# Another order of a unit's seven products in the last projection and in the unit in front of it, and the first block's sample matmuls in groups of four

## The chip, the cores and the metric

The kernel runs on one core of a Trainium2 chip. The metric is the device time of one execution in microseconds (us). One core has five engines that run side by side, each with its own queue of instructions: TensorE (PE, matrix products), VectorE (DVE), ScalarE (ACT), GpSimd (POOL) and SyncE (SP, which here issues most transfers). They wait for one another through semaphores. Matrix products are accumulated in banks of PSUM; everything else lies in SBUF, which has 128 partitions.

## The reference: what is computed

One inference step of one decoder layer, in fp32, for a prompt of 2048 tokens and, with the same weights, for 32 sample tokens (8 sequences of 4). The model width is 1024, the hidden width of the feed-forward part 2816.

```python
def decoder_layer(x, s_gla, s_ssm, conv_buf, mk, mv, lw):
    m, s_gla, s_ssm, conv_buf = mixer(rmsnorm(x, lw['ln_mix_pre']), s_gla, s_ssm, conv_buf, lw)
    h = x + rmsnorm(m, lw['ln_mix_post'])
    a = cross_attend(rmsnorm(h, lw['ln_xa_pre']), mk, mv, lw['w_xq'], lw['w_xo'])
    h = h + rmsnorm(a, lw['ln_xa_post'])
    hf = rmsnorm(h, lw['ln_ffn_pre'])
    f = (jax.nn.silu(hf @ lw['w_gate']) * (hf @ lw['w_up'])) @ lw['w_down']
    h = h + rmsnorm(f, lw['ln_ffn_post'])
    return h, s_gla, s_ssm, conv_buf
```

`mixer` is one large projection (`hn @ w_in`), gated linear attention on one half of the channels, a state-space scan (SSD, with a decay per head and chunk) on the other, and an output projection. `cross_attend` attends over 256 memory tokens. The outputs are both groups of tokens and the new states.

## The kernel before

**Products.** Every fp32 product is made of three matmuls on halves: each operand is split into a high part (a rounded copy, made by ScalarE) and a low part (the rest, a subtraction on VectorE), and `three` (lines 133 to 136) adds high x high (line 134), high x low (135) and low x high (136) into one PSUM bank.

**First half (0 to 857 us).** Four blocks of 512 tokens go through the input projection, the attention heads and the scan. `wload` (line 120) loads a raw piece of weights of 128 x 1024 on SP's queue into one of two `wraw` buffers and splits it into `whi` and `wlo`. `tm(n)` is one of three projections with tokens in the rows: four weight pieces (`u`), each with 24 matmuls of 512 columns. In the first block (`has_s`) the 32 sample tokens ride along: behind each piece come two sample matmuls, which take the raw, unsplit weights, and which lie in different column groups of TensorE (`tile_position=(0, g0)`):

```python
                if has_s:
                    for kk in range(2):
                        kt = 2 * u + kk
                        g0 = (kt % 4) * 32
                        nc.tensor.matmul(psv[g0:g0 + 32], lhsT=sx[:, kt], rhs=wr[:, kk * 512:(kk + 1) * 512],
                                         start=kt < 4, stop=kt >= 4, tile_position=(0, g0))
```

The scan's running decays are transposed into a tile of 16 rows (`lcT`) and spread by a mask (`bmask`) into rows 0 to 15 of an operand `R`, by GpSimd. `junk` is a scratch tile that takes squares whose sums alone are wanted.

**Second half (857 to 2833 us).** Here stand the other projections as passes over units: o, s and v (attention, 8 units each), three passes g (gate and up projection, 22 units each; the third with two row tiles and the samples, 272 columns), and three passes d (the last projection, 8 units each: parts of 3, 4 and 4 pairs of row tiles of the hidden width, so 384, 512 and 512 columns wide). GD is the first d pass, XG the first g pass.

A unit is a 2 x 2 block product by seven products instead of eight (Strassen and Winograd's form). Product 0 is p0, 1 is C11, 2 is p2, 3 is p3, 4 is C22, 5 is C12, 6 is C21; p0, p2, C22 and C21 go to the two buffers of bank `accA`, C11 to `accB`, p3 and C12 to `accC`. Their order is TURN = [0, 1, 3, 2, 5, 4, 6], and a list `order`, written out once, holds all products of all units. The last product of a unit stands behind the first of the next one, but ahead of it where XG or GD begins:

```python
    for n, (k, _, _) in enumerate(work):
        first = [(n, 0)]
        if n:
            first.insert(0 if begins[n] and k in (XG, GD) else 1, (n - 1, 6))
        order += first + [(n, i) for i in TURN[1:6]]
```

- *The moving side of a unit.* Its raw tile is loaded two units ahead (`load_unit`). Four products ahead of a product its operand is prepared: `Unit.hi` makes the sums S1, S2, S4 and S3 on VectorE (line 1644) where a product needs one (S1 with product 1, though product 3 reads it), the high part on ScalarE (line 1662); the low part (VectorE, line 1664) follows one product later.
- *The weights of a pass.* `Pieces` brings them in pieces of one or two per product, in the order of `flat`, which follows TURN. A piece is loaded into a staging buffer `st` (three of them), split on ScalarE (line 1731) and VectorE (line 1735), and lies in one of seven rooms of a ring, one room per product, taken in turn. A room is taken again only once the product of the pass before that lies in it is through in that pass's last unit (`inside`, `spent`; `larger` returns without work otherwise). One piece is made per product beside the last unit of the pass before, and then beside the first unit of the new one; a product whose weights are not there makes them first (`while i not in held[n].full: held[n].step()`).
- *Evictions.* What a product leaves in PSUM is copied or added into rows in SBUF: g passes at line 1991 (with ScalarE at line 1984 for the sigmoid part), d passes in `evac_d` (VectorE, line 2038, or a copy on ScalarE). In a d pass a row tile's store, or in the last part its final norm, is issued when the later one of its halves is there: for the first half of the rows (m = 0) at C12, for the second at C21.
- In the first unit of GD, eight sample matmuls at a time stand between two products (line 2082).

Of the kernel before, what the change touches and what calls it, by code (L numbers as in the profile page):

```python
# [12 lines left out]
F32 = mybir.dt.float32  # L13
F32R = mybir.dt.float32r
I32 = mybir.dt.int32
AF = mybir.ActivationFunctionType
# [26 lines left out]
def hymba_kernel(ctx: ExitStack, tc: tile.TileContext, a: dict, o: dict, dbg: dict | None = None):  # L43
# [17 lines left out]
    def mxt():  # L61
        return mx.tile([P, 512], F32, name="mx")
# [55 lines left out]
    last = [None]  # L118

    def wload(src, pieces=1, pool=None, raws=None):  # L120
        raw = (raws or wp).tile([P, 1024], F32, name="wraw", bufs=2)
        nc.sync.dma_start(out=raw, in_=src)
        hi, lo = ((pool or wp).tile([P, 1024], F32R, name=n, bufs=1 if pool else 3) for n in ("whi", "wlo"))
        w = 1024 // pieces
        with tc.high_priority(offset=AHEAD):
            for c in range(pieces):
                cs = slice(c * w, (c + 1) * w)
                last[0] = nc.scalar.activation(hi[:, cs], raw[:, cs], AF.Copy)  # L128
                nc.vector.tensor_tensor(lo[:, cs], raw[:, cs], f(hi)[:, cs], op=ALU.subtract)  # L129
        return raw, hi, lo  # L130
# [200 lines left out]
    nc.vector.memset(Sg, 0.0)  # L331
    Ss = pstate.tile([P, 512], F32, name="Ss")
    nc.vector.memset(Ss, 0.0)
    bmask = pstate.tile([16, 8], F32, name="bmask")
    nc.vector.tensor_tensor(bmask, ident[:16, 0:8], ident[:16, 8:16], op=ALU.add)
    sps = pstate.tile([96, BT], F32R, name="sps")
    nc.gpsimd.memset(f(sps), 0.0)
    rmask = pstate.tile([P, BT], F32, name="rmask")
# [183 lines left out]
    def block(b):  # L522
# [31 lines left out]

        def fm_narrow(u):

            raw = wp.tile([P, 1024], F32, name="wraw", bufs=2)
            nc.sync.dma_start(out=raw, in_=a["w_in_fm"][u])
            both = wp.tile([P, 1024], F32R, name="whi", bufs=3)
            nc.scalar.activation(both, raw, AF.Copy)  # L560
            k_c = lambda t: t.rearrange("p (k c) -> p k c", c=P)
            nc.vector.tensor_tensor(k_c(both)[:, :, 64:104], k_c(raw)[:, :, 0:40], k_c(f(both))[:, :, 0:40], op=ALU.subtract)
            pss = [acct() for _ in segs]
            for kt in range(KT):
                for si, (n0, n1) in enumerate(segs):
                    for part, x in enumerate((xh, xl)):
                        nc.tensor.matmul(pss[si][:, :n1 - n0], lhsT=both[:, kt * P:(kt + 1) * P], rhs=x[kt][:, n0:n1],
                                         start=kt == 0 and part == 0, stop=kt == KT - 1 and part == 1)
            return pieces(pss)
# [24 lines left out]
                beside()  # L594


        sp = pa.tile([40, BT], F32, name="sp")
        for pp, lo, hi, of_s in fm_narrow(12):
            dst = s_sp if of_s else sp[:, lo:hi]
            nc.scalar.copy(dst, pp[0:40])  # L600
            nc.vector.tensor_tensor(dst, pp[64:104], dst, op=ALU.add)
            if has_s:
                nc.vector.tensor_tensor(dst, dst, rb[:40, BT:T] if of_s else rb[:40, lo:hi], op=ALU.mult)
# [8 lines left out]
        lc, ll = lcl[:, 0:32], lcl[:, 32:64]  # L612
        wl_ = pa.tile([P, 96], F32, name="wl_")
        wdec, ell, elc = (wl_[:, 32 * i:32 * i + 32] for i in range(3))
        lcT = pa.tile([16, BT], F32, name="lcT")

        def decays():
            ps = mxt()
# [64 lines left out]
        def tm(n):  # L683

            ps = [acct() for i in range(4)]
            psv = mxt() if has_s else None
            for u in range(4):
                wr, wh, wl = wload(a["w_in_tm"][n, u])
                for i in range(4):
                    for kk in range(2):  # L690
                        kt = 2 * u + kk
                        three(ps[i], xh[kt][:, i * P:(i + 1) * P], xl[kt][:, i * P:(i + 1) * P],
                              wh[:, kk * 512:(kk + 1) * 512], wl[:, kk * 512:(kk + 1) * 512], kt == 0, kt == KT - 1)
                    if i % 2 == 0 and "pa2" not in late:
                        step(back)
                if has_s:
                    for kk in range(2):
                        kt = 2 * u + kk
                        g0 = (kt % 4) * 32
                        nc.tensor.matmul(psv[g0:g0 + 32], lhsT=sx[:, kt], rhs=wr[:, kk * 512:(kk + 1) * 512], start=kt < 4, stop=kt >= 4,  # L700
                                         tile_position=(0, g0))
                if u < 3:
                    beside(False)
            return ps, psv
# [59 lines left out]
        def ssd_first(c):  # L764
            cs = slice(c * CH, (c + 1) * CH)

            R = Rs[0]
            nc.gpsimd.tensor_tensor(out=R[0:16], in0=lcT[:, cs].unsqueeze(1).broadcast_to([16, 8, CH]),
                                    in1=bmask.unsqueeze(2).broadcast_to([16, 8, CH]), op=ALU.mult)
            M = pa.tile([P, 8, CH], F32, name="M")  # L770

            px = mxt()
# [32 lines left out]
        def ssd_second(c, M, xdt, xw, xD, Bt):  # L805
            cs = slice(c * CH, (c + 1) * CH)
            pi = mxt()
            for g in range(2):
                nc.tensor.matmul(pi[:, g * 256:(g + 1) * 256], lhsT=xc[6 + g][:, cs], rhs=Ss[:, g * 256:(g + 1) * 256], start=True, stop=True)
            py = mxt()  # L810
            for h in range(8):
                nc.tensor.matmul(py[:, h * 64:(h + 1) * 64], lhsT=M[:, h], rhs=xdt[:, h * 64:(h + 1) * 64], start=True, stop=True)
            y = pa.tile([P, 512], F32, name="y")
            nc.vector.tensor_tensor(v3(y), v3(pi), elc[:, c * 8:(c + 1) * 8].unsqueeze(2).broadcast_to([P, 8, 64]), op=ALU.mult)
            nc.gpsimd.tensor_tensor(out=xD, in0=xD, in1=y, op=ALU.add)
            nc.vector.tensor_tensor(xD, py, xD, op=ALU.add)
            y = z_[:, c]
            nc.gpsimd.tensor_tensor(out=y, in0=xD, in1=y, op=ALU.mult)

            pS = mxt()  # L820
            for g in range(2):
                nc.tensor.matmul(pS[:, g * 256:(g + 1) * 256], lhsT=Bt[:, g * P:(g + 1) * P], rhs=xw[:, g * 256:(g + 1) * 256], start=True, stop=True)
            nc.vector.tensor_tensor(v3(Ss), v3(Ss), ell[:, c * 8:(c + 1) * 8].unsqueeze(2).broadcast_to([P, 8, 64]), op=ALU.mult)
            nc.vector.tensor_tensor(Ss, Ss, pS, op=ALU.add)

            ss = small.tile([P, 8], F32, name="ss")
            for g in range(2):
                junk = pa.tile([P, 256], F32, name="junk")
                nc.scalar.activation(junk, y[:, g * 256:(g + 1) * 256], AF.Square, accum_out=ss[:, g:g + 1])
            rs = rstd_of(ss[:, 0:2], "rs", 256, cols=2)  # L830
            for g in range(2):
                nc.vector.tensor_scalar(y[:, g * 256:(g + 1) * 256], y[:, g * 256:(g + 1) * 256], rs[:, g:g + 1], None, op0=ALU.mult)
            return y
# [794 lines left out]

    TURN = [0, 1, 3, 2, 5, 4, 6]

    class Unit:

        def __init__(self, src, n):
            self.w = n * P
            self.q = src(praw.tile([P, 2048], F32, name="raw", bufs=2))
            self.t, self.got = {}, {}

        def op(self, out, x, y, o):  # L1640
            t, q = self.t, self.q
            t[out] = pf.tile([P, 512], F32, name="sum", bufs=2)[:, 0:self.w].rearrange("p (k c) -> p k c", c=P)
            x, y = (q[i] if isinstance(i, int) else t[i] for i in (x, y))
            nc.vector.tensor_tensor(t[out], x, y, op=o)  # L1644

        def hi(self, i):

            if i == 1:
                self.op("S1", 2, 3, ALU.add)
            if i == 3:  # L1650
                self.op("S2", "S1", 0, ALU.subtract)
# [43 lines left out]
    class Pieces:  # L1695
# [2 lines left out]

        def __init__(self, k, loads, w, ahead, wide=False):
            self.k, self.w, self.at, self.full, self.wide = k, w, {}, set(), wide  # L1700
            self.flat = [(i, n + 1 == len(loads[i]), ld) for i in TURN for n, ld in enumerate(loads[i])]
            self.n, self.lo, self.q = 0, None, deque()
            for _ in range(ahead):
                self.load()
# [320 lines left out]
    def evac_d(p, j, y, h):  # L2025
# [4 lines left out]
        def ev(name, ps):  # L2030
# [12 lines left out]
                nc.vector.tensor_tensor(t, t, half(gain["ln_ffn_post"])[n], op=ALU.mult)  # L2043
            elif final and not (h and name == "C21"):
                later.append(lambda: nc.scalar.activation(mxt(), t, AF.Square, accum_out=ss[m][:, n:n + 1]))
            if name in ("C12", "C21"):
                if h:
                    posts.append(after_last(j, m, y[m], ss[m], h[m]))
                elif final:
# [79 lines left out]
    def load_unit(n):  # L2129
        if n < len(work):  # L2130
            k, g, _ = work[n]
            kind, i, _ = passes[k]
            units[n] = unit_g(*g) if kind == "g" else unit_d(i, g) if kind == "d" else unit_x({"o": mixT, "s": xq, "v": pT}[kind], g)

    def enter(k):

# [54 lines left out]


    order = []
    for n, (k, _, _) in enumerate(work):
        first = [(n, 0)]
        if n:
            first.insert(0 if begins[n] and k in (XG, GD) else 1, (n - 1, 6))
        order += first + [(n, i) for i in TURN[1:6]]
    order.append((len(work) - 1, 6))
    NAMES = {0: "p0", 1: "C11", 2: "p2", 3: "p3", 4: "C22", 5: "C12", 6: "C21"}  # L2200
    fctx = ctx.enter_context(ExitStack())
# [227 lines left out]
```

## Time and profile before

| quantity | value |
|---|---|
| time, median of 3 runs | 2836.76 us (2830.9 to 2837.76) |
| the profiled execution's own time | 2833.82 us |
| its span | 2832.1 us |
| granted TensorE clock, mean | 0.993 |
| busy: TensorE matmuls / weight loads | 97% / 84% |
| busy: VectorE / ScalarE / GpSimd | 73% / 52% / 19% |
| bytes moved | 514.27 MB, mean 182 GB/s |

By stretches of the span (microseconds, TensorE's busy time in each):

| stretch | what runs | length | TensorE busy |
|---|---|---|---|
| 0 to 283 | first block of 512 tokens, with the samples | 283 | 268.25 |
| 283 to 857 | blocks two to four | 574 | 565.81 |
| 857 to 1380 | passes o, s, v | 523 | 505.26 |
| 1380 to 2345 | passes g | 965 | 939.53 |
| 2345 to 2400 | end of the last g pass, first units of d | 55 | 49.43 |
| 2400 to 2653 | d, up to its last part | 253 | 249.73 |
| 2653 to 2833 | d, last part | 180 | 163.48 |

How the views are read: rows of a timeline give the start, the duration, the engine, the line, the operation and the tiles (written <- read), the shapes and how many equal records were joined; in square brackets stands the idle time before the instruction and what ended it. Rows of the waits give the engine, its tile and line, whom it waited for, then the total, the number and the longest wait. Rows of groups give busy time and the mean of one in ns, and the idle time before. Rows of windows give the stretch and its length, then the busy time and the number of instructions of TensorE, of its weight loads, VectorE, ScalarE and GpSimd, the granted clock (1.00 is full), the share of the DMA engines and GB/s.

### The profile page before, as it was taken

The page shows a single profiled execution, that of the slowest core. Times are in us where ns is not written, and L with a number is a line of the kernel's source. Part 1 is how long each engine was busy: PE and PEld are TensorE (multiplying, and loading weights), DVE is VectorE, ACT ScalarE, POOL GpSimd, SP SyncE. Part 2 cuts the span into 40 slices and gives each one's busy share as a digit, 9 for nine tenths or more (in the row PEclk, how much of TensorE's full clock was granted, in tenths as well). Part 3 has the DMA queues.
Part 4 walks back from the last instruction along what each step waited for, and adds up shares of the span by engine and source line. Part 5 has one row for each costly group of instructions (what it writes and reads, how often), then busy time and mean ns, then how long its engine had stood idle before and what let it go on. Part 6 is the DMA issues. An engine that isn't in the chain of part 4 may idle for free.

```text
span 2832.1 us, 41818 instructions
## 1 busy us (share of the span) xinstructions
PE 2741.5 (97%) x15207; PEld 2365.1 (84%) x15207; DVE 2070.8 (73%) x3830; ACT 1478.9 (52%) x2929; POOL 526.9 (19%) x719
## 2 busy tenths in 40 slices
PE   8999999999998999999899999999999999999998
PEld 8887878787786878878799888899999997778786
DVE  7676677776757787677888787668677788564676
ACT  4445554544546787777755434434445555353432
POOL 2132332321321321015321210001000000000011
PEclk9999999999999999999999999999999999999999
DMA  7345535343266886468865567774244436565865
GB/s 246 120 127 187 153 99 167 119 131 90 82 208 226 292 280 225 149 189 250 268 218 182 186 237 240 256 253 166 95 155 163 144 127 208 186 208 106 243 150 133
DMA packets 151678, 514.27 MB, mean 182 GB/s; under 512 B 18240, under 2 KB 29552, under 8 KB 137904
## 3 DMA queue, kind: packets, MB, share of 16 engines
q1 hardware_dynamic: 94560, 331.81, 35.6%
q0 software_dynamic: 44816, 154.92, 17.3%
q10 hardware_dynamic: 12096, 24.86, 2.6%
q8 instruction: 120, 1.97, 0.3%
q14 instruction: 86, 0.70, 0.1%
HBM read 365.76 MB, written 145.76 MB: 181 GB/s over the span
## 4 chain that ended last, share of the span: by engine, by line
PE 71%; DVE 10%; ACT 5%; DMA 3%; issue 3%; POOL 1%; DVEq 0%; POOLq 0%; ACTq 0%; SPq 0%
PE accA L134 9%; PE accA L135 9%; PE accA L136 9%; PE accC L134 5%; PE accC L135 5%; PE accC L136 5%; PE acc L134 4%; PE acc L135 4%; PE acc L136 4%; PE accB L134 2%; PE accB L136 2%; PE accB L135 2%; DVE s L1664 2%; ACT r L1731 1%; DVE sum L1644 1%
## 5 line engine op out<-in xcount | busy, mean ns | idle before, releaser
L134 PE MATMUL accA<-r,s 128*128 128x512 f32 (+2 forms) x1792 | 637.1, 356 | 21.5 <-ACT r L1731 6.9
L136 PE MATMUL accA<-r,s 128*128 128x512 f32 (+2 forms) x1792 | 628.3, 351 | 1.5 <-DVE s L1664 1.5
L135 PE MATMUL accA<-r,s 128*128 128x384 f32 (+2 forms) x1472 | 502.4, 341 | 1.7 <-DVE r L1735 1.7
L134 PEld LDWEIGHTS accA<-r,s 128*128 128x128 f32 x1792 | 338.4, 189 | 75.1 <-issue 12.2
L1662 ACT ACTIVATE s<-sum 128x512 fp32r<-128x512 f32 (+1 forms) x456 | 282.5, 620 | 211.9 <-DVE sum L1644 103.2
L136 PEld LDWEIGHTS accA<-r,s 128*128 128x128 f32 x1792 | 338.8, 189 | 32.4 <-DVE s L1664 2.3
L134 PE MATMUL accC<-r,s 128*128 128x512 f32 (+2 forms) x896 | 320.4, 358 | 13.2 <-ACT s L1662 4.0
L1664 DVE TENSOR_TENSOR s<-sum,s 128x512 fp32r<-128x512 f32 (+1 forms) x456 | 304.8, 675 | 20.2 <-ACT s L1662 19.9
L136 PE MATMUL accC<-r,s 128*128 128x512 f32 (+2 forms) x896 | 315.4, 352 | 0.0
L135 PEld LDWEIGHTS accA<-r,s 128*128 128x128 f32 x1472 | 278.8, 189 | 18.6 <-DVE r L1735 2.6
L1664 DVE TENSOR_TENSOR s<-raw,s 128x512 fp32r<-128x512 f32 (+1 forms) x342 | 231.9, 678 | 51.6 <-ACT s L1662 50.6
L135 PE MATMUL accC<-r,s 128*128 128x384 f32 (+2 forms) x736 | 252.3, 343 | 0.8 <-DVE r L1735 0.8
L1662 ACT ACTIVATE s<-raw 128x512 fp32r<-128x512 f32 (+1 forms) x342 | 213.2, 624 | 68.2 <-PE accC L136 48.9
L128 ACT ACTIVATE whi<-wraw 128x1024 fp32r<-128x1024 f32 (+2 forms) x140 | 128.6, 934 | 182.5 <-PE acc L135 101.2
L134 PEld LDWEIGHTS accC<-r,s 128*128 128x128 f32 x896 | 170.4, 190 | 41.8 <-ACT s L1662 8.6
L129 DVE TENSOR_TENSOR wlo<-wraw,whi 128x1024 fp32r<-128x1024 f32 (+2 forms) x140 | 154.7, 1115 | 53.0 <-ACT whi L128 52.4
L136 PEld LDWEIGHTS accC<-r,s 128*128 128x128 f32 x896 | 170.3, 190 | 15.5 <-DVE s L1664 0.3
L134 PE MATMUL acc<-xh,whi 128*128 128x512 f32 (+1 forms) x464 | 168.5, 364 | 9.2 <-ACT xh L289 9.1
L142 POOL TENSOR_TENSOR rs<-ms,nhalf 128x1 f32<-128x1 f32 (+4 forms) x125 | 109.7, 879 | 348.7 <-DVE ms L140 332.4
L136 PE MATMUL acc<-xh,wlo 128*128 128x512 f32 (+1 forms) x464 | 164.9, 357 | 1.7 <-DVE wlo L129 1.7
L135 PE MATMUL acc<-xl,whi 128*128 128x512 f32 (+1 forms) x464 | 164.6, 356 | 0.2 <-DVE xl L290 0.2
L1644 DVE TENSOR_TENSOR sum<-raw 128x512 f32<-128x512 f32 (+1 forms) x228 | 155.3, 681 | 3.6
(697 smaller groups left out, 5868.7 us busy)
## 6 DMA issues: line engine op xcount, KB each, us to landing
raw<-in_w_gu_dram SPq DMA_DIRECT2D x66, 1024.0 KB, 4.9
wraw<-in_w_in_fm_dram SPq DMA_DIRECT2D x52, 512.0 KB, 3.6
wraw<-in_w_in_tm_dram SPq DMA_DIRECT2D x48, 512.0 KB, 3.7
st<-in_w_down_dram SPq DMA_DIRECT2D x37, 512.0 KB, 6.5
aT<-og POOLq DMA_DIRECT2D x22, 768.0 KB, 4.7
yp<-y POOLq DMA_DIRECT2D x32, 512.0 KB, 6.9
raw<-aT SPq DMA_DIRECT2D x16, 1024.0 KB, 6.3
out_y_dram<-y POOLq DMA_DIRECT2D x28, 512.0 KB, 5.9
```

Of the source, the lines that this page charges most:

```text
L128: last[0] = nc.scalar.activation(hi[:, cs], raw[:, cs], AF.Copy)
L129: nc.vector.tensor_tensor(lo[:, cs], raw[:, cs], f(hi)[:, cs], op=ALU.subtract)
L134: nc.tensor.matmul(ps, lhsT=wh, rhs=ah, start=start, stop=False, skip_group_check=more)
L135: nc.tensor.matmul(ps, lhsT=wh, rhs=al, start=False, stop=False, skip_group_check=more)
L136: nc.tensor.matmul(ps, lhsT=wl, rhs=ah, start=False, stop=stop, skip_group_check=more)
L142: nc.gpsimd.tensor_tensor(out=rs[:rows, :cols], in0=ms[:rows, :cols], in1=nhalf[:rows, :cols], op=ALU.pow)
L1644: nc.vector.tensor_tensor(t[out], x, y, op=o)
L1662: nc.scalar.activation(h3, v, AF.Copy)
L1664: return lambda: nc.vector.tensor_tensor(l3, v, f(h3), op=ALU.subtract)
L1731: nc.scalar.activation(hi, v, AF.Copy)
```

## The change

- The seven products of a unit get a second order, TURN_D = [0, 3, 2, 5, 4, 1, 6], in which C11 comes sixth. It holds for all units of the d passes but the very last one, and for the last unit of the last g pass, the unit in front of them. The weights of the d passes are brought in that order. In these units S1 is made with product 0.
- In a d pass the first half of the rows (m = 0) is now complete at C11, so its store or final norm is issued there, but in the very last unit, which keeps the old order, at C12.
- In `tm` the sample matmuls of two weight pieces are issued together, four at a time, behind every second piece; the raw piece of the even step is held until then. `wraw` gets a third buffer, except in the memory part's own pool.
- Places in SBUF: `lcT` becomes rows 64 to 79 of the tile `sp`, and `bmask` and the rows of `R` that it fills move to the same partitions; `junk` shares the tile `y`.

```diff
     def wload(src, pieces=1, pool=None, raws=None):
-        raw = (raws or wp).tile([P, 1024], F32, name="wraw", bufs=2)
+        raw = (raws or wp).tile([P, 1024], F32, name="wraw", bufs=2 if raws else 3)
...
-        lcT = pa.tile([16, BT], F32, name="lcT")
+        lcT = sp[64:80]
...
-                if has_s:
-                    for kk in range(2):
-                        kt = 2 * u + kk
+                raws.append(wr)
+                if has_s and u % 2:
+
+                    for kt in range(2 * u - 2, 2 * u + 2):
                         g0 = (kt % 4) * 32
-                        nc.tensor.matmul(psv[g0:g0 + 32], lhsT=sx[:, kt], rhs=wr[:, kk * 512:(kk + 1) * 512], start=kt < 4, stop=kt >= 4,
-                                         tile_position=(0, g0))
+                        nc.tensor.matmul(psv[g0:g0 + 32], lhsT=sx[:, kt], rhs=raws[kt // 2][:, kt % 2 * 512:(kt % 2 + 1) * 512],
+                                         start=kt < 4, stop=kt >= 4, tile_position=(0, g0))
...
-            nc.gpsimd.tensor_tensor(out=R[0:16], in0=lcT[:, cs].unsqueeze(1).broadcast_to([16, 8, CH]),
-                                    in1=bmask.unsqueeze(2).broadcast_to([16, 8, CH]), op=ALU.mult)
+            nc.gpsimd.tensor_tensor(out=R[64:80], in0=lcT[:, cs].unsqueeze(1).broadcast_to([16, 8, CH]),
+                                    in1=bmask[64:80].unsqueeze(2).broadcast_to([16, 8, CH]), op=ALU.mult)
...
-            y = pa.tile([P, 512], F32, name="y")
+            y = junk = pa.tile([P, 512], F32, name="y")
...
     TURN = [0, 1, 3, 2, 5, 4, 6]
 
+    TURN_D = [0, 3, 2, 5, 4, 1, 6]
...
+            self.s1 = 1
...
-            if i == 1:
+            if i == self.s1:
                 self.op("S1", 2, 3, ALU.add)
...
-            self.flat = [(i, n + 1 == len(loads[i]), ld) for i in TURN for n, ld in enumerate(loads[i])]
+            self.flat = [(i, n + 1 == len(loads[i]), ld) for i in (TURN_D if passes[k][0] == "d" else TURN) for n, ld in enumerate(loads[i])]
...
-            if name in ("C12", "C21"):
+            if name == "C21" or name == ("C12" if h else "C11"):
...
+            if turn(n) is TURN_D:
+                units[n].s1 = 0
...
+    def turn(n):
+
+        k, _, left = work[n]
+        return TURN_D if (passes[k][0] == "d" or k + 1 == GD and left == 1) and n + 1 < len(work) else TURN
+
     for n, (k, _, _) in enumerate(work):
...
-        order += first + [(n, i) for i in TURN[1:6]]
+        order += first + [(n, i) for i in turn(n)[1:6]]
```

More of the change, by code (lines that the diff above doesn't have):

```diff
@@ L333, in hymba_kernel @@
     nc.vector.memset(Ss, 0.0)
-    bmask = pstate.tile([16, 8], F32, name="bmask")
-    nc.vector.tensor_tensor(bmask, ident[:16, 0:8], ident[:16, 8:16], op=ALU.add)
+    bmask = pstate.tile([P, 8], F32, name="bmask")
+    nc.vector.tensor_tensor(bmask[64:80], ident[64:80, 64:72], ident[64:80, 72:80], op=ALU.add)
     sps = pstate.tile([96, BT], F32R, name="sps")
@@ L555, in fm_narrow @@
         def fm_narrow(u):
-            raw = wp.tile([P, 1024], F32, name="wraw", bufs=2)
+            raw = wp.tile([P, 1024], F32, name="wraw", bufs=3)
             nc.sync.dma_start(out=raw, in_=a["w_in_fm"][u])
@@ L594, in block @@
                 beside()
-        sp = pa.tile([40, BT], F32, name="sp")
+        sp = pa.tile([P, BT], F32, name="sp")
         for pp, lo, hi, of_s in fm_narrow(12):
-            dst = s_sp if of_s else sp[:, lo:hi]
+            dst = s_sp if of_s else sp[0:40, lo:hi]
             nc.scalar.copy(dst, pp[0:40])
@@ L686, in tm @@
             psv = mxt() if has_s else None
+            raws = []
             for u in range(4):
@@ L827, in ssd_second @@
             for g in range(2):
-                junk = pa.tile([P, 256], F32, name="junk")
-                nc.scalar.activation(junk, y[:, g * 256:(g + 1) * 256], AF.Square, accum_out=ss[:, g:g + 1])
+                nc.scalar.activation(junk[:, g * 256:(g + 1) * 256], y[:, g * 256:(g + 1) * 256], AF.Square, accum_out=ss[:, g:g + 1])
             rs = rstd_of(ss[:, 0:2], "rs", 256, cols=2)
```

## The prediction

> **What bounds the kernel now.** I read the page first, then a table of stretches, then the waits of TensorE in the stretches that the change touches, and last the timelines of single queues there.
>
> ```profile
> span 2832.1 us, 41818 instructions
> ...
> 0.00:283.00 283.00, 268.25 (x1758) 233.46 (x1758) 199.44 (x391) 139.19 (x250) 73.09 (x100) 1.00 0.53 170
> 2345.00:2400.00 55.00, 49.43 (x287) 41.93 (x286) 46.59 (x83) 31.27 (x58) 2.54 (x4) 0.97 0.71 248
> 2400.00:2653.00 253.00, 249.73 (x1100) 197.97 (x1099) 141.75 (x224) 102.83 (x175) 19.94 (x29) 1.00 0.59 173
> ```
>
> TensorE bounds almost everywhere: in the last projection (2400 to 2653) it is busy 249.73 of 253 us with VectorE at 56%. The join into that projection (2345 to 2400) is the exception: VectorE is busy 46.59 of 55 us. So in steady state a change of order gains nothing, and only the joins can move. These are TensorE's waits there:
>
> ```profile
> PE accA L134 <- DVE t L1991: 4.8, 1, 4.8
> PE accC L134 <- ACT s L1662: 4.0, 1, 4.0
> PE accA L134 <- DVE y L2038: 2.2, 4, 0.9
> ...
> PE accC L134 <- ACT t L1984: 0.5, 1, 0.5
> ```
>
> **Part 1: first block's samples in fours.** Twelve pairs of sample matmuls become six fours (three projections of four weight pieces each).
>
> ```profile
> 142.34 0.40 PE L135 MATMUL acc<-wlo,xh 128*128 128x512 f32 x1
> 142.57 0.40 PE L136 MATMUL acc<-whi,xl 128*128 128x512 f32 x1
> 142.91 1.05 PE L700 MATMUL mx<-wraw,sx 128*32 128x512 f32 x4
> 143.89 0.74 PE L134 MATMUL acc<-whi,xh 128*128 128x512 f32 x2
> ...
> 2376.85 0.39 PE L136 MATMUL accA<-r,s 128*128 128x512 f32 x1
> 2377.16 1.07 PE L2082 MATMUL mx<-e,s_f 128*32 128x512 f32 x8
> 2378.16 0.50 PE L134 MATMUL accB<-r,s 128*128 128x512 f32 x1
> 2378.50 0.39 PE L135 MATMUL accB<-r,s 128*128 128x512 f32 x1
> ```
>
> A pair shows as four records. From the matmul in front to the one behind it takes 143.89 - 142.57 = 1.32 us, against 0.23 us between two ordinary matmuls (142.34 to 142.57): 1.09 us, and the next spacing is 0.34 in place of 0.23, so about 1.2 us. A four (eight records, the samples of the last projection, line 2082) takes 2378.16 - 2376.85 = 1.31 us: the same. Six fewer groups are -7.2 us. TensorE is the bound there (268.25 of 283 busy), so most of it counts. Against it: the raw piece of an even step is now held until the odd step is over, so the fourth piece's load starts only there, and what covers it is one step without sample matmuls, 24 x 0.23 = 5.5 us, against a load (its row), a split on ScalarE and one on VectorE; of these splits the only wait of TensorE in the third projection is this one:
>
> ```profile
> 254.37 5.11 DMA wraw<-in_w_in_tm_dram
> ```
>
> ```profile
> PE acc L135 <- DVE wlo L129: 0.3, 1, 0.3
> ```
>
> The splits' rows are those of the later join, the same operations at the same size:
>
> ```profile
> L1735 DVE TENSOR_TENSOR r<-st,r 128x1024 fp32r<-128x1024 f32 x7 | 8.6, 1223 | 6.2 <-ACT r L1731 6.2
> ...
> L1731 ACT ACTIVATE r<-st 128x1024 fp32r<-128x1024 f32 x7 | 7.3, 1049 | 3.2 <-DMA st<-wT 3.2
> ```
>
> Load and both splits are 5.11 + 1.05 + 1.22 = 7.4 us: in the third projection, where little else runs between the steps, one wait grows from 0.3 by 7.4 - 5.5 = 1.9 us at most, and I take +1.2. I take -6, ends -7.2 and -3. The third raw buffer lets the other blocks load earlier; no wait of TensorE on a split of theirs exceeds the 0.3 just shown, so nothing, but since it also shifts addresses and the order of loads, 0 with ends -3 and +3 for all stretches outside the joins. The moved rows (decays in partitions 64 to 79 of another tile) and the scratch that now shares the y tile change no count or size: nothing; the scratch's write stands behind the same chunk's sum in any case.
>
> **Part 2: the order at the join.** Call L the unit in front, D the first unit of the last projection, E the second. Before, TensorE ran L0 . L1 L3 L2 L5 L4 L6 D0 D1 D3 ...; L6 stood right behind L4, whose eviction from the same bank was late:
>
> ```profile
> 2358.39 0.29 PE L134 MATMUL accB<-r,s 128*128 128x272 f32 x1
> 2359.91 0.29 PE L134 MATMUL accC<-r,s 128*128 128x272 f32 x1
> ...
> 2363.60 1.22 DVE L1735 TENSOR_TENSOR r<-st,r 128x1024 fp32r<-128x1024 f32 x1
> 2364.74 0.68 DVE L1664 TENSOR_TENSOR s<-sum,s 128x512 fp32r<-128x512 f32 x1
> 2365.34 0.68 DVE L1735 TENSOR_TENSOR r<-st,r 128x512 fp32r<-128x512 f32 x1
> 2365.94 0.68 DVE L1664 TENSOR_TENSOR s<-raw,s 128x512 fp32r<-128x512 f32 x1
> ...
> 2371.85 0.43 PE L134 MATMUL accA<-r,s 128*128 128x272 f32 x1 [4.84 <-DVE t L1991]
> 2374.56 0.63 PE L134 MATMUL accA<-r,s 128*128 128x512 f32 x1
> ```
>
> A product of L takes 1.52 us. VectorE's starts give what each step occupies: a large weight piece 1.14 (2363.60 to 2364.74), a low part of L, 512 columns, 0.60 (to 2365.34), a small piece 0.60 (to 2365.94). By columns I take 0.47 for a low part or a sum of D (384), 0.60 for an eviction of D (512) and, for L's eviction with its two followers (272 + 256 + 16), 0.90. VectorE has more than 1.52 us of this per product, because the weights of D are split beside L, one piece per product: a low part, a sum and a piece are already 1.8 to 2.3.
>
> Now the new order, L0 . L3 L2 L5 L4 L1 L6 D0 D3 D2 D5 D4 D1 E0 D6. Behind L4 stands L1, so L6 has a product of cover. But the pieces go into a ring of seven places in the order of products, and a place is free when L has run the product that lies in it. L's weights lie in the old order, D's come in the new: D's second product (D3) belongs in the place of L1, which now runs sixth. So behind D0's two pieces no piece is made during L3, L2, L5 and L4. With those four left out, 3.5 us in all, VectorE comes to L4's eviction near 2365.1, and L6 can start without a wait at 2355.37 + 7 x 1.515 = 2365.97 (2358.39 less two products is 2355.37). It ends at 2367.5; before, at 2374.6 (the first matmul at 512 columns).
>
> Then twelve pieces are left for eight products, and from D5 on half of them are made by force right in front of their product. Walking the queues (D's product 9 x 0.228 = 2.05; its eviction 0.60 plus 0.13 to notice; each load as below, three buffers in flight):
>
> ```profile
> 2362.22 4.45 DMA st<-wT
> 2382.39 6.61 DMA st<-wT
> ```
>
> D0 runs from 2367.5 to 2369.5. D3's second piece is split by about 2371.9 only, behind its first, so D3 waits 0.8 and ends 2372.4. D2's second piece is ready near 2374.6; D2 waits 1.5, ends 2375.9. The load of D5's first piece starts behind D3's second split; it lands 4.45 us on, takes 1.05 on ScalarE and 1.14 on VectorE: about 2379.1. D5 waits 3.2, ends 2381.2. D4's piece stands in VectorE's queue behind D5's eviction (0.13 + 0.60), a low part (0.47) and its own 1.14: D4 waits 2.3, ends 2385.5. D1 has a sum more in front: 2.7, ends 2390.3. E0 has its weights. D6 waits 0.9. Together 11.4 us. What goes: 4.84 + 0.5 (the two waits in L) and the half clock behind the first, below, 1.7 us: -7.0. The two groups of samples among D's products (1.1 us each, the x8 rows) fall partly into the new waits: -1, ends 0 and -2.2.
>
> The clock is a term by itself:
>
> ```profile
> 873.60:877.00 3.40, 1.47 (x6) 0.90 (x6) 1.74 (x4) 2.75 (x6) 0.00 (x0) 1.00 0.69 231
> 877.00:880.40 3.40, 3.37 (x7) 2.36 (x8) 3.16 (x5) 3.33 (x5) 0.00 (x0) 0.50 0.41 139
> 2512.80:2516.20 3.40, 2.14 (x9) 1.42 (x8) 2.79 (x5) 3.32 (x5) 0.00 (x0) 1.00 0.59 174
> 2371.80:2375.50 3.70, 3.65 (x15) 3.47 (x16) 3.28 (x8) 1.27 (x3) 0.00 (x0) 0.54 0.48 159
> ```
>
> After 3.4 us with 1.47 busy the next 3.4 ran at 0.50; with 2.14 busy they did not. A stretch at 0.50 costs up to 3.4 x 0.5 = 1.7 us. D5 and D1 wait 2.4 to 2.7 us within such a stretch, so I take two, one partly idle: +2.7, ends 0 and +5.1. The join: 11.4 - 7.0 - 1 + 2.7 = +6, ends -1 (the pieces wait for one another less than I let them, no half clock) and +12.
>
> The Trainium skill, page "TensorE: Matmul & The Clock Gate", section "HAM oscillation — how this bites in real kernels", asks for no idle gap over some 3.4 us. Less than 2 us of idle in all were followed by 0.50 in the first two rows above, so this trace sets the point lower than that rule does.
>
> **The two joins inside the projection.** There the ring and the pieces have the same order, so no place is late. The C22 eviction gets a product of cover: the four waits on y (2.2 us) include the one at the very end (0.9), where the last unit keeps the old order; -1.2 at most. In exchange the first row half's store comes two products later, close to the second's, among loads that are already slow (the 4.0 us wait on s stands behind such a load), and C12 no longer ends a row. -0.5, ends -4 and +4.
>
> **Sum.** -6 + 6 - 0.5 + 0 = -0.5 against the profiled execution's 2833.82 (its span and 1.7 around it), that is 2833.3; that execution lies 2.9 under the median of the runs, 2836.76. I predict 2836.
>
> **Rivals.** (a) The backlog is absorbed: VectorE waits for ScalarE between D's pieces, so it had room there (6.2 us on the large pieces' row above). If D's pieces cost no wait, the join is -7 and the sum -6 - 7 - 0.5: 2823; half of it, 2829. Against: a product of D then needs an eviction, a low part and 1.7 us of pieces in 2.05. 0.21.
> (b) Slower: the loads. If D's pieces land after 6.6 us (second load row) rather than 4.45, each of D5, D4, D1 and D6 waits up to 2.1 us more, since three buffers admit no earlier start: +8.4, sum +8: 2845. It decides from about 6 us on; for it, 248 GB/s are moved in that stretch; against, L's four products without pieces leave the queues emptier. 0.16.
> (c) The fours gain nothing, because every gain comes back as a wait for the held piece: 2842. Against: outside the third projection other work stands between the steps. 0.08.
> (d) The clock stays whole: D's waits of 2.3 to 3.2 us have products of 2.05 between them, so each 3.4 us may hold 2 us of work, as the third row above did without a slower clock after it, and the 2.7 go: 2833. Against: 1.47 of 3.4 is reached wherever 1.9 us of one wait lie in one such stretch. 0.10. The Trainium skill's rule on idle gaps, named above, would give this case too.
>
> **Chances.** The forecast has 0.45. Under 0.3% (8.5 us) a measurement of this kernel tells little from no change. Faster: (a) and a little of the forecast's lower end, 0.25. Slower: half of (b) and the upper end of the forecast, 0.14. Same: 0.61. The forecast's own range is 2829 to 2843; with most of (a) and (b), 2825 to 2845.
>
> **What would show it.** Sample groups in the first 283 us: six of eight records, about 1.3 us each. L6 starts without the 4.84 us wait. Between L0's pieces and L1 no weight piece on VectorE; then waits of TensorE on r at D3, D2, D5, D4, D1, the longest 2 to 3 us at D5 to D1, with one or two stretches at 0.50. At the inner joins, no wait of accA on y but at the end. I am wrong if D's products follow one another every 2.05 us, or if the first block does not get shorter by 4 to 7 us.

## The result, and the profile after

The changed kernel takes 2841.7 us (median of 11 runs, 2839.23 to 2847.62) against 2833.85 us (11 runs of before, 2830.8 to 2837.76). The ratio is 1.003, 95% interval 1.0022 to 1.0037: slower by 6 to 10 us, where 2836 was forecast, 0.8 us below the 2836.76 that was then known of before, and "same" as the likeliest outcome (0.61). The time lies in the forecast's own range (2829 to 2843), near its upper end, but the kernel became slower and not faster: each of its runs is above each run of before.

The profiled execution has a span of 2838.9 us, 6.8 more than before. Where it goes is read from the starts of TensorE at places that both orders share: the first product of the second half (line 134, tile accA), then the second product of L, of the third d unit, of the last part's first unit, and the last unit's second product. First column the start, then the duration. In the changed kernel the lines behind the first change stand further down: 1735 of before is 1740 here, 1731 is 1736, 2038 is 2043. Before (L's row is in the prediction, 2358.39):

```profile
857.36 0.48 PE L134 MATMUL accA<-r,s 128*128 128x512 f32 x1
...
2409.91 0.39 PE L134 MATMUL accB<-r,s 128*128 128x512 f32 x1
...
2662.65 0.40 PE L134 MATMUL accB<-r,s 128*128 128x512 f32 x1
...
2805.10 0.40 PE L134 MATMUL accB<-r,s 128*128 128x512 f32 x1
```

After:

```profile
853.33 0.48 PE L134 MATMUL accA<-r,s 128*128 128x512 f32 x1
...
2352.36 0.29 PE L134 MATMUL accC<-r,s 128*128 128x272 f32 x1
...
2414.44 0.39 PE L134 MATMUL accC<-r,s 128*128 128x512 f32 x1
...
2665.57 0.40 PE L134 MATMUL accC<-r,s 128*128 128x512 f32 x1
...
2811.93 0.40 PE L134 MATMUL accB<-r,s 128*128 128x512 f32 x1
```

| stretch | difference at its end | change in it | forecast |
|---|---|---|---|
| first half | -4.0 | -4.0 | -6 |
| passes o to g, up to L | -6.0 | -2.0 | 0 |
| L and the first two d units | +4.5 | +10.6 | +6 |
| the rest of parts one and two | +2.9 | -1.6 | about 0 |
| join into the last part, and that part | +6.8 | +3.9 | about -0.5 |

These are single executions, and the experiments below left twelve more traces to compare with. The third row stands out: this stretch takes 51.5 us before and 62.1 after, and 49 to 51 in every trace without late rooms. The other changes behind the first half do not. Passes o to g take 1498 to 1505 us over all traces, the rest of parts one and two 250 to 253, and the last stretch, 142.5 before and 146.4 after, takes 142.4 to 147.0 in the traces that have the old order there and no extra matmuls.

At the join of the g and d passes the waits are those that were forecast. After, TensorE from 2345 to 2400 (total, number, longest):

```profile
PE accA L134 <- ACT r L1736: 4.4, 3, 2.6
PE accA L135 <- DVE r L1740: 2.5, 4, 0.8
PE accC L134 <- ACT r L1736: 2.0, 1, 2.0
PE accB L135 <- DVE r L1740: 0.8, 1, 0.8
PE accC L135 <- DVE r L1740: 0.8, 1, 0.8
PE accB L134 <- ACT r L1736: 0.6, 1, 0.6
```

All are waits on r, the weights of D, 11.1 us in all, and the wait of accA on t (L6, 4.84 us) is gone. Why the weights are late stands in VectorE's own timeline: after D0's second piece (the second row) there is no weight piece (line 1740) for 8 us; the next one, for D3, is taken up only once L1 has run (2358.41 to 2359.92).

```profile
2353.12 1.23 DVE L1740 TENSOR_TENSOR r<-st,r 128x1024 fp32r<-128x1024 f32 x1 [0.38 <-ACT r L1736]
...
2354.86 0.68 DVE L1740 TENSOR_TENSOR r<-st,r 128x512 fp32r<-128x512 f32 x1
...
2362.93 1.22 DVE L1740 TENSOR_TENSOR r<-st,r 128x1024 fp32r<-128x1024 f32 x1
```

What was not foreseen in full is the clock. Windows of 3.4 us (TensorE's busy time is the first number behind the length, the granted clock stands behind the five engines):

```profile
2370.20:2373.60 3.40, 0.93 (x3) 0.19 (x1) 1.21 (x2) 2.47 (x4) 0.00 (x0) 1.00 1.01 352
2373.60:2377.00 3.40, 3.07 (x7) 2.48 (x8) 0.88 (x2) 0.00 (x0) 0.00 (x0) 0.50 0.93 334
2377.00:2380.40 3.40, 1.04 (x4) 0.26 (x2) 2.51 (x4) 1.99 (x3) 0.00 (x0) 0.99 0.22 83
2380.40:2383.80 3.40, 3.40 (x8) 2.33 (x8) 0.48 (x1) 0.00 (x0) 0.00 (x0) 0.51 0.66 187
...
2394.10:2397.50 3.40, 1.25 (x4) 0.85 (x5) 2.77 (x5) 1.24 (x3) 0.00 (x0) 1.00 0.45 181
2397.50:2400.90 3.40, 3.40 (x9) 2.63 (x9) 1.15 (x2) 1.01 (x2) 0.56 (x1) 0.50 0.39 159
```

After windows with 0.93, 1.04 and 1.25 us of work the next one runs at half clock; after the one from 2383.80, with 2.01, it does not. That makes three slow windows at this join, against one before.

The join into the last part has more slow windows too. There TensorE waits for an eviction into y that stands on VectorE behind a late weight piece:

```profile
PE accC L134 <- DVE y L2043: 3.6, 1, 3.6
PE accA L134 <- ACT r L1736: 1.4, 1, 1.4
```

Mean granted clock from 2655 to 2715, before and after: 0.97 and 0.91. At half clock that is 60 x 0.03 x 2 = 3.6 us, one window, before, and 60 x 0.09 x 2 = 10.8 us, three windows, after; half of the difference, some 3.4 to 3.6 us, would be nearly all of the 3.9 that this join lost. The waits themselves do not differ: the rows add up to 5.6 us before (4.0 of them the wait on s that the prediction shows) and 5.8 after.

```profile
2655.00:2715.00 60.00, 54.44 (x228) 43.26 (x227) 47.49 (x72) 26.80 (x48) 6.54 (x9) 0.97 0.77 219
```

```profile
2655.00:2715.00 60.00, 54.22 (x214) 42.80 (x213) 44.57 (x65) 26.42 (x44) 4.55 (x6) 0.91 0.72 214
```

### The profile page after: what moved, and what is told of

Its sections match the earlier page's. It is cut to its first block, busy times and chain, and to the rows that moved or that the text cites. A ratio compares the mean times of both kernels' runs of the same rounds, so it can differ in the third digit from the quotient of the medians.

```text
span 2838.9 us, 41856 instructions
## 1 busy us (share of the span) xinstructions
PE 2743.6 (97%) x15207; PEld 2367.3 (83%) x15207; DVE 2073.8 (73%) x3830; ACT 1476.7 (52%) x2929; POOL 529.3 (19%) x719
```

## The experiments

**The parts by themselves.** `order_only` is before with the two orders alone, `samples_only` before with everything of the change ahead of the second half, `buffer_only` the same without the fours (third raw buffer and moved tiles, with pairs).

> Before plus the new orders alone (no fours, two raw buffers, tiles where they were). Theory (late rooms: D3's weights belong in the room of L1, which runs sixth, so no piece is made during L3, L2, L5, L4; the waits of D follow from that): the trace of the changed kernel lost 10.5 us at the join of the g and d passes and 3.9 at the last inner join, so this one is 10 to 14 us above before: 2844 to 2848. Rival (the loss comes with the shifted loads of the first half, the third raw buffer): no more than 3 us above before, 2837 at most.

> Before plus the fours, the third raw buffer and the moved tiles alone, old orders everywhere. Theory: the first block is 4 us shorter as in the changed kernel's trace, all else as before: 2829 to 2831. Rival (the fours gain nothing in the end, since later waits take it back): 2833 to 2835.

> Before plus the third raw buffer and the moved tiles, with pairs as before. Theory (the fours carry the gain of the first half): within 2 us of before, so 2834 to 2837 on the chip of the last runs. Rival (the third buffer carries it): 5 us below before, about 2830, as with the fours.

Measured: order_only 2845.59 us and samples_only 2830.45 against 2835.64 of before on the same chip (ratios 1.0035, 1.0021 to 1.0048, and 0.9979, 0.9970 to 0.9988); buffer_only 2832.26 against 2832.98 (0.9994, 0.9986 to 1.0003). So the order costs about 10 us and the sample part gains about 5. The buffer's part of that gain is not told from nothing, though its interval allows 4 us; resampling the runs (drawing from them again and again; the bounds hold 95%), samples_only lies 4.7 us (2.3 to 7.1) below buffer_only, each beside its own before. The traces tell it otherwise: with the third buffer and pairs the first half of buffer_only's one execution ends at 853.38, as early as with the fours (851.1 to 854.8 in eleven traces; 857.4 and 856.2 without both), and TensorE's waits up to 283 us add up to 11.3 us, against 14.5 before. So that the fours bring gain is shown by the times alone, and how it divides stays open.

**Is it the order, or the rooms?** `front_unit_old` leaves L in the old order, so that its rooms come free in the order in which D's weights go into them:

```diff
-        return TURN_D if (passes[k][0] == "d" or k + 1 == GD and left == 1) and n + 1 < len(work) else TURN
+        return TURN_D if passes[k][0] == "d" and n + 1 < len(work) else TURN
```

`same_room` keeps the new order in L too, and gives a product's weights the room of the same product of the pass before:

```diff
-                k = made[0] % 7
+                k = next((r for r, v in inside.items() if v == (self.k - 1, i)), made[0] % 7)
```

> The changed kernel with the old order in the unit in front (L) and the new one in the d passes. Theory (late rooms): the rooms come free in the order in which D's pieces go into them, so the waits of D (11.1 us in the changed kernel) go and L6's single wait of some 4.8 us is back: 8 to 11 us below the changed kernel, 2831 to 2834. Rival (the new order inside the d units costs by itself, whatever L does): within 3 us of the changed kernel, 2839 or more.

> The changed kernel, but a product's weights take the room of the same product of the pass before instead of the next in turn, so that rooms come free in L's own order. Theory (late rooms): one piece per product is made during L3 to L1 again, the waits of D on its weights all but go, and L6 keeps its product of cover: 9 to 14 us below the changed kernel, 2828 to 2832. Rival (VectorE has no room for the pieces beside L in any order, so a wait of 4 us or more stays on L6 or D): 2834 or more. Rival (order itself): 2839 or more.

Measured on the same chip as order_only and samples_only: front_unit_old 2828.6 us, below the range expected for it, and same_room 2828.88, inside its range, ratios 0.9979 (0.9969 to 0.9988) and 0.9978 (0.9968 to 0.9987). One line that moves no work takes away the whole loss, and so does the old order in L with the new one in the d passes: the late rooms were the cause, and the order inside the d units was not. The waits at the join, same_room:

```profile
PE accA L134 <- DVE t L1996: 2.8, 1, 2.8
PE accA L135 <- DVE r L1740: 0.6, 1, 0.6
```

and front_unit_old:

```profile
PE accA L134 <- DVE t L1996: 4.4, 1, 4.4
PE accC L134 <- ACT t L1989: 0.5, 1, 0.5
```

With the old order L6 waits as before; with the new one its product of cover takes 1.6 us off (4.4 to 2.8), about one product of L (1.52). The rival of same_room is right in that a wait stays on L6, though it is below the 4 us that it named. Beside samples_only (2830.45) the two are lower by 1.9 and 1.6 in the medians, which these runs do not tell from nothing. The traces do show a small gain at the join: with the rooms mended and the new order in L, L and the first two d units take 49.2 us here and 48.9 to 50.2 in the further traces of that kind, against 51.0 to 51.5 in the four with the old order in L.

**What the slow clock costs.** `filled_waits` is the changed kernel, late rooms and all, with 32 matmuls whose result nothing reads, placed at D's waits (the first number of a pair ahead of the product, the second ahead of its last group):

```diff
+        fill = {2: (4, 0), 5: (8, 0), 4: (8, 0), 1: (4, 0), 6: (0, 8)}.get(i, (0, 0)) if k == GD and begins[n] else (0, 0)
...
+                nc.tensor.matmul(e_, lhsT=sh[:, 0:P], rhs=held[n].moving(0, 0)[0], start=True, stop=True)
```

> The changed kernel with 32 extra matmuls of 512 columns (0.23 us each, their result is not used) in front of or inside products D2, D5, D4, D1 and D6 of the first d unit, where TensorE waits for weights. Theory (the three stretches at half clock at that join come from the waits and cost 1.4 to 1.7 us each): two or three of them go, the extra matmuls lie in the waits, and the time is 2 to 5 us below the changed kernel, so 2 to 6 us above before. Rival (the slow stretches cost nothing, since the weights are late anyway): no change against the changed kernel, 7 to 10 us above before. Rival (the extra matmuls delay the products): 10 us or more above before.

Measured: 2835.82 against 2832.98 us, ratio 1.0009 (1.0000 to 1.0018), where the changed kernel has 1.003: as the theory expected. More work in the same place made it some 6 us faster (resampled, 3.3 to 8.3, each beside its own before), and the granted clock of its runs is 0.9925 in the mean, against 0.9892 in the changed kernel's. At the join of the one traced execution the clock is whole:

```profile
2350.00:2405.00 55.00, 50.06 (x270) 39.41 (x270) 41.73 (x73) 28.93 (x53) 1.83 (x3) 1.00 0.66 221
```

The changed kernel had 0.92 there:

```profile
2345.00:2400.00 55.00, 43.87 (x221) 33.53 (x220) 40.21 (x69) 27.63 (x51) 1.84 (x3) 0.92 0.62 210
```

In that trace L and the first two d units take 58.3 us, 3.8 less than the 62.1 of the changed kernel. The three slow windows are therefore worth somewhat less there than three times 1.7. (The traced execution is the slowest of its eleven, 2841.74 us; it lost its time in front of L, where passes o to g took 1504.7 us.)

**The join into the last part.** `first_part_only` is same_room with the new order in L and the first part alone, its last unit in the old one. `late_store` is same_room with the two row stores of the second part's last unit issued five products later.

> The changed kernel with a product's weights in the room of the same product of the pass before, and the new order in L and the units of the first part of d alone (all but its last unit); parts two and three in the old order. Theory (the late rooms were one loss, and the new order at the last inner join is a second one of 2 to 4 us): 2 to 4 us below the 2829 of the kernel with the same rooms, 2825 to 2827, with one stretch at half clock at the last inner join in place of two. Rival (the inner joins differ from run to run and not by order): 2828 to 2830.

> The changed kernel with the same rooms, and the two row stores of the second part's last unit issued five products later, behind the loads of the next weights. Theory (in the new order these two stores lie 3.5 us apart in place of 6.7 and slow the loads of the last part's weights to 9 to 10 us, which costs the 2 to 4 us at that join): the loads there land in 4 to 7 us and the time falls by 2 to 5 us against the same rooms, to 2824 to 2827. Rival (the queue of VectorE, not the loads, is late there): no change, 2828 to 2830.

Measured: first_part_only 2825.54 us, ratio 0.9975 (0.9964 to 0.9985), and late_store 2830.23, 0.9988 (0.9979 to 0.9996), both against 2832.98. late_store did not do what it says: its first store starts 5.7 us after the start of C11 in the trace, and 5.6 in same_room. Nothing else stands in GpSimd's queue there, so it comes to the store as soon as the row is complete, wherever the program puts it; late_store says nothing on its question. `late_store_2` therefore puts a one-column copy in front, which reads an operand made five products later:

```diff
+                nc.gpsimd.tensor_copy(small.tile([P, 8], F32, name="late")[:, 0:1], f(units[n4].got[i4][0])[:, 0:1])
```

> As the kernel with the held-back stores, but with a GpSimd copy in front of each store that reads an operand made five products later, so that GpSimd's queue really comes to the stores later. Theory (the two stores slow the loads at the last inner join, and with them its waits): the loads of the last part's first weights land in 4 to 7 us in place of 9 to 10, the waits and half clock there (8.8 us in the trace with the same rooms) shrink to 3 to 6, and the time is 2 to 5 us below the kernel with the same rooms in this job. Rival (VectorE's queue is late there in any case, or other transfers fill the place): no difference beyond 2 us.

Beside it stand same_room once more, and the kernel of first_part_only once more (under the name first_part_filled, though nothing is filled in it):

> The kernel with the same rooms once more, on the chip of the two others of this job, to compare with. Theory: 4 to 7 us below before, as in its first job.

> The kernel with the new order in L and the first part alone (same rooms), without extra matmuls, beside the kernel with the same rooms on the same chip. Theory (the new order at the inner joins costs 2 to 4 us): 2 to 4 us below the kernel with the same rooms. Rival (no difference by order): within 1.5 us.

Measured, before at 2832.65: late_store_2 2825.95, ratio 0.9975 (0.9964 to 0.9985); same_room_2 2829.98, 0.9987 (0.9978 to 0.9996); first_part_filled 2828.49, 0.9981 (0.9970 to 0.9991). The gain of same_room_2, 2.7 us in the medians, is smaller than the 4 to 7 expected. Resampling the runs of these three, late_store_2 is 4.3 us below same_room_2 in the mean (95%: 1.9 to 6.5), and first_part_filled 1.3 (1.5 above to 4.1 below). So the two stores do slow this join in the new order, but what the order itself costs there is not told from nothing. The four loads of weights that start beside the stores in same_room_2 (from 2651 to 2663 us; KB each, median us to landing):

```profile
st<-wT SPq DMA_DIRECT2D x2, 512.0 KB, 8.8
yp<-y POOLq DMA_DIRECT2D x2, 512.0 KB, 8.5
st<-in_w_down_dram SPq DMA_DIRECT2D x2, 512.0 KB, 6.5
```

The same four in late_store_2, where the stores come later (from 2648.5 to 2660 us):

```profile
st<-wT SPq DMA_DIRECT2D x2, 512.0 KB, 6.4
st<-in_w_down_dram SPq DMA_DIRECT2D x2, 512.0 KB, 4.1
```

These loads became as fast as was expected, 4 to 7 us in the medians. The wait of accC on y (2.3 us in same_room_2) is gone, and in late_store_2's trace no window at half clock lies at this join.

This join can be as slow in the old order. In buffer_only and first_part_filled, which both have the old order there, TensorE waits 7.0 and 7.7 us for one operand, three windows run at half clock, and the last stretch takes 146.3 and 147.0 us, as much as the 146.4 of the changed kernel. No run moves the stores in the old order. Buffer_only, from 2649 to 2709 us (line 1661 makes the high part of an operand):

```profile
PE accC L134 <- ACT s L1661: 7.0, 1, 7.0
```

**A version that beats both.** `filled_best` is first_part_only with 64 extra matmuls at waits that its trace shows.

```diff
+        if k == 0 and begins[n]:
+            fill = {3: 8, 5: 8, 6: 4}.get(i, 0)
+        elif k + 1 in (XG, GD) and left == 1 and i == 6:
+            fill = 12 if k + 1 == XG else 18
+        elif k == GD + 2 and begins[n] and i == 5:
+            fill = 14
```

> The kernel with the new order in L and the first part alone, plus 64 extra matmuls (their result is not used) placed where its trace shows TensorE waiting: 20 in the first unit of the second half (products 3, 5 and 6), 12 ahead of the last product of pass v, 18 ahead of L6, 14 ahead of product 5 of the last part's first unit. Theory (a stretch at half clock follows a wait and costs 1.4 to 1.7 us, and work without use in the wait keeps the clock whole): three to five stretches go, and the time is 4 to 8 us below the kernel without them. Rival (the waits have other ends, so that the extra matmuls only delay): 0 to 5 us above it.

Measured: 2819.07 us, ratio 0.9955 to before (0.9942 to 0.9967), and 7.8 us below the same kernel without them in the mean (4.9 to 10.7). The first unit of the second half, the join of g and d and the last join, without the extra matmuls (first_part_filled):

```profile
850.00:905.00 55.00, 42.47 (x165) 31.39 (x165) 36.84 (x54) 30.03 (x54) 7.62 (x10) 0.94 0.56 201
2340.00:2380.00 40.00, 37.57 (x248) 32.80 (x247) 36.48 (x67) 25.14 (x46) 1.43 (x2) 1.00 0.74 246
2640.00:2700.00 60.00, 50.64 (x205) 39.85 (x204) 41.38 (x58) 26.07 (x43) 4.56 (x6) 0.91 0.71 204
```

and with them:

```profile
850.00:905.00 55.00, 48.78 (x196) 36.72 (x195) 38.58 (x55) 31.21 (x57) 5.45 (x9) 0.97 0.57 203
2340.00:2380.00 40.00, 39.08 (x244) 32.84 (x242) 34.91 (x63) 26.05 (x47) 1.43 (x2) 1.00 0.73 244
2640.00:2700.00 60.00, 57.36 (x246) 45.55 (x245) 48.38 (x73) 27.63 (x49) 6.55 (x9) 1.00 0.77 219
```

At the last join the three slow windows are gone, and in the first unit one remains of two (0.94 and 0.97 of 55 us). At the join of g and d this trace had a whole clock without them too; the trace of first_part_only had two slow windows there. Over all runs the granted clock is 0.995 in the mean, against 0.992 without the extra matmuls.

## Why the prediction was right and wrong

- *The mechanism of the join* was right: no pieces during L3 to L4, no wait on L6, then waits on r at D's products, and what goes (7.0). The sum of the waits came out right too, 11.4 forecast and 11.1 in the rows, but in part by luck. D3 did not wait (0.8 forecast); D2, D5, D4 and D1 waited 1.0, 2.8, 2.4 and 1.4 us (1.5, 3.2, 2.3 and 2.7 forecast); D6 waited 3.5 in place of 0.9. The walk of the queues left out what else stands in ScalarE's queue. There D6's second piece (the last row) stood behind a step of the sample rows, which waited 2.61 us for VectorE:

```profile
2394.72 0.59 ACT L2098 ACTIVATE mx<-m 32x512 f32<-32x512 f32 x1 [2.61 <-DVE m L149]
2395.26 0.18 ACT L2098 ACTIVATION_READ_ACCUMULATOR mx<-m 32x1 f32 x1
2395.35 0.61 ACT L1736 ACTIVATE r<-st 128x512 fp32r<-128x512 f32 x1
```

D4's pieces, too, stand on ScalarE, from 2377.98 on, behind the high part of another operand (2377.55) that starts right behind the end of D5 (2377.46); the prediction had them held up on VectorE. No row gives the 0.13 us in which VectorE was to notice the end of a product.
- *The clock term* is the step that failed. Two windows at half clock were put in, one of them partly idle (+2.7); there were three, nearly filled with work, which by the prediction's own price is +5.1, its far end. One of the three stands behind D6's wait. The waits themselves were a little dearer than the rows say: in the middle of D4 the second matmul stands 1.26 us behind the first, 1.03 more than the usual 0.23, where the idle time is 0.76; six such waits on line 135 make 11.1 into about 12.6. And the -1 for the samples brought nothing beyond that: their first group stood between D0 and D3, where nothing was awaited, and what the second saved, ahead of D1, is already in the 11.1. Together 12.6 - 7 + 5.1 = 10.7 for +6; the trace has 10.6, inside the ends given (-1 to +12). Of the 7.3 us by which the trace (+6.8) missed the sum (-0.5), this join is 4.6; the last join is 4.4, and the other stretches together -1.6.
- *The joins inside the projection* (-0.5, ends -4 and +4): no clock term stood there at all, and the join into the last part had two windows at half clock more than before. The prediction named the later store beside slow loads and left it unpriced; late_store_2 shows that place, and a size of about 4 us. But two traces with the old order there are as slow, so that the 3.9 come from the new order is not shown. Nor is the -1.6 between 2414 and 2665 told from the scatter of that stretch.
- *The fours.* The sample part as a whole was sized right: -6 forecast, -5.2 in the times. The six groups of eight records stand in the trace, 1.32 to 1.33 us from neighbour to neighbour, and so does the wait that they bring in the third projection, on the high part (0.3 + 1.2 forecast on the low part, which shows 0.5):

```profile
PE acc L134 <- ACT whi L128: 1.5, 1, 1.5
```

The "nothing" for the third buffer left out the waits of the first block, which fall by 3.2 us in buffer_only's trace; in the times it is not contradicted.
- *The rivals.* (a), the absorbed backlog, fell: D's products did not follow one another every 2.05 us. (b), slow loads, has a time (2845) not far from the measured one, but the waits came another way. (d), the whole clock, is what filled_waits made by hand; what it is worth there is some 6 us in the times (3.3 to 8.3) and 3.8 in the trace, not the 2.7 that it was priced at. The Trainium skill, page "TensorE: Matmul & The Clock Gate", section "HAM oscillation — how this bites in real kernels", tells of idle gaps over about 3.4 us; none of D's waits reached that (2.6 at most), and the clock still fell, so the measurement decides. Its next section, "A second HAM failure mode: psum-queue depth-cycling", tells of short, frequent idle times that also toggle the clock, and this trace agrees with that one (0.93 us of work in 3.4, then 0.50).

## What to carry to other kernels

Where a ring of buffers is refilled in turn, an order that its user changes and its filler doesn't (or the other way round) stalls the filler for as long as one early room is late: tie the room to what lies in it, not to a counter. Price a chain of short waits by window and not by wait: each 3.4 us with little work was followed here by 3.4 us at half clock, a loss of up to 1.7 us more, and matmuls of no use placed into such waits gave time back (7.8 us in one kernel that was otherwise the same). Compare one stretch over several traces before its difference is put down to a change: the last join moved by over 4 us between traces with the same order there. And a transfer that is put later in the program is not later on an idle queue: to delay it, something ahead of it in its queue has to wait.

## What the runs showed of the hardware that was not expected

In the traces of before and after, read in windows of 3.4 us that begin and end with the slow ones, every window at full clock behind the first 10 us in which TensorE worked for 1.7 us or less was followed by one at half clock, and none in which it worked for 1.9 us or more was; of two in between, with 1.77 and 1.79, one was. Extra work on the busiest engine shortened the kernel twice, by some 6 us with 32 matmuls and by 7.8 us with 64; the granted clock rose with it, from 0.989 to 0.9925 and from 0.992 to 0.995 in the mean of the runs. Four sample matmuls in four column groups took as long as two (1.07 us for the eight records of a four, 1.05 for the four of a pair). And four loads of 512 KB that started beside two accumulating row stores of 512 KB took 8.8 and 6.5 us (medians of two each); with the stores moved behind them, 6.4 and 4.1 us.
